# Rotating 96 images by 90 degrees: 2 MB loads of whole slabs, and neighbouring slabs stored together

## The chip, the cores and the metric

The kernel runs on one core of a Trainium2 chip. A core has a vector engine (DVE), a scalar engine (ACT), a queue engine that issues transfers (SP), and 16 DMA engines that move data between device memory (HBM) and the on-chip memory SBUF, which has 128 partitions. A second on-chip memory, PSUM, can be written and read by DVE and ACT but not by DMA. The metric is the device time of one execution in microseconds (us); less is better. A slab in this text is 2 MB of rows.

## The reference

```python
def setup_inputs():
    batch, c, h, w = 32, 3, 256, 256
    return {"x": np.random.randn(batch, c, h, w).astype(np.float32)}

def reference(x: np.ndarray) -> np.ndarray:
    return np.rot90(x, k=-1, axes=(-2, -1)).astype(np.float32)
```

Each of the 96 images of 256 x 256 float32 values is turned by a quarter clockwise. Nothing is calculated: 25.17 MB are read, put into another order, and 25.17 MB are written.

## The kernel before

The 24,576 image rows are cut into 12 slabs of 2048 rows, eight images each. All twelve slabs stay in SBUF at once, each in a *unit*: 16 KB in every one of the 128 partitions.

A transfer lays several consecutive rows of 1 KB into one partition. There are two layouts. *Short* is 8 rows, so 8 KB in one piece, and a slab is two such pieces per partition, one from each half of the slab (index `i`). *Long* is 16 rows, 16 KB in one piece; here a half of the slab goes to every second partition (`i::2`, 64 of them).

DVE's 32x32 block transpose with a rearranged source and destination (L118) does the turning, in two instructions of 128x2048 values for one slab. It turns what is read short into what is written long, and the other way round; a third form takes two units in the long layout at once, in four instructions. Slabs 0, 1 and 2 are loaded short and stored long; slabs 3 to 7 are loaded long and stored short; 8 with 9 and 10 with 11 are loaded and stored long. Slabs 1 and 2 are loaded by one transfer of 2 MB each, all others by halves of 1 MB, and the first half of slab 11 is cut once more, into 14 KB and 2 KB rows.

A turn does not write into its own unit. `home = [turned0] + units[:last]` (L100): slab n is turned from unit n into unit n-1, which the turn before has set free, and slab 0 goes to PSUM (`turned0`). At the end ACT copies `turned0` into the last unit (L146), and slab 0 is stored from there, as the last store of the program (`store(0)`, L148). The pairs 8/9 and 10/11 move likewise: the turn of the pair 8/9 writes into the tile of units 3 and 7, that of 10/11 into the tile of 8/9.

A unit is a tile of its own, except that three tiles hold two units each (L72: 3 with 7, 8 with 9, 10 with 11), so that a paired turn can address both. Waits between instructions are not written by hand: the framework derives them from which tile regions an instruction reads and writes.

All transfers are issued by SP, in program order: all loads first (L88, L92, L96), then the stores. The stores of slabs 4, 3, 5, 6, 7, 1, 2 follow, the first of them held back by hand until the 14 KB piece of slab 11's load has landed (L139), so that stores do not start among the loads. After that each paired turn is followed by its stores (L124, L127), and slab 0 comes last (L130). L124 stores slab 8 (and later 10), both halves, in one transfer of 2 MB from the 64 even partitions, two pieces of 16 KB each that lie 1 MB apart in the output; slabs 9 and 11 follow from the odd partitions in halves of 1 MB (L127). The short stores (L132) are of 2 MB, the long ones of slabs 0, 1 and 2 (L130) of 1 MB. SP has eight completion semaphores for its transfers in use, and a transfer waits until the one eight places before it has landed.

Of the kernel before, what the change touches and what calls it, by code (L numbers as in the profile page):

```python
# [1 line left out]

# [4 lines left out]

@with_exitstack
def kernel(
    ctx: ExitStack,
    tc: tile.TileContext,
    x: bass.AP,
    out: bass.AP,
):

    nc = tc.nc
    fp32 = mybir.dt.float32

    B, C, H, W = x.shape
    P = nc.NUM_PARTITIONS
    RL, RS = 16, 8  # L50
    I = 2
    Q = P * RS // H
    n_slabs = B * C // (Q * I)
    last = n_slabs - 1
    F = RS * W
    long_st = (0, 1, 2)
    both = (8, 10)
    paired = [n + a for n in both for a in range(2)]

    rows_in = x.rearrange("b c h w -> (b c h) w")  # L60
    rows_out = out.rearrange("b c h w -> (b c h) w")

    def short(rows):
        return rows.rearrange("(n i p r) w -> n p i (r w)", i=I, p=P, r=RS)

    def long(rows):
        return rows.rearrange("(n i m r) w -> n i m (r w)", i=I, m=P // I, r=RL)

    ld_short, ld_long, st_short, st_long = short(rows_in), long(rows_in), short(rows_out), long(rows_out)

    units = [None] * n_slabs
    adjacent = [(3, 7), (8, 9), (10, 11)]  # L72
    pairs = []
    for us in adjacent + [(u,) for u in range(n_slabs) if all(u not in us for us in adjacent)]:
        pool = ctx.enter_context(tc.tile_pool(name=f"unit{us[0]}", bufs=1))
        held = pool.tile([P, len(us), I * F], fp32, name=f"u{us[0]}")
        for j, u in enumerate(us):
            units[u] = held[:, j]
        pairs.append(held)
    psum = ctx.enter_context(tc.tile_pool(name="psum", bufs=1, space=bass.MemoryType.PSUM))  # L80
    turned0 = psum.tile([P, I * F], fp32, name="turned0")

    def fours(t):
        return t.rearrange("p (i f) -> p i f", i=I)

    for n in (0, 1, 2, 3, 7, 4, 5, 6, *range(8, n_slabs)):
        if n in (1, 2):
            nc.sync.dma_start(out=fours(units[n]), in_=ld_short[n])  # L88
            continue
        for i in range(I):  # L90
            if n in long_st:
                ld = nc.sync.dma_start(out=fours(units[n])[:, i], in_=ld_short[n][:, i])  # L92
            else:
                cuts = (0, 14 * W, RL * W) if (n, i) == (last, 0) else (0, RL * W)
                for f0, f1 in zip(cuts, cuts[1:]):
                    ld = nc.sync.dma_start(out=units[n][i::I, f0:f1], in_=ld_long[n, i][:, f0:f1])  # L96
                    if f1 == 14 * W:
                        mark = ld

    home = [turned0] + units[:last]  # L100

    def turn(n):
        if n in long_st:
            src = fours(units[n]).rearrange("p i (r g c) -> p c r g i", r=RS, c=RL)
            dst = home[n].rearrange("p (c k r) -> p c r k", c=RL, r=RS)[:, :, ::-1, ::-1]
            parts, step = 2, RL // 2
        elif n in paired:
            if n not in both:
                return
            src = pairs[both.index(n) + 1].rearrange("p a (r g c) -> p c r g a", r=RL, c=RL)  # L110
            dst = pairs[both.index(n)].rearrange("p i (c k r) -> p c r k i", c=RL, r=RL)[:, :, ::-1, ::-1, :]
            parts, step = 4, RL // 4
        else:
            src = units[n].rearrange("p (r g c) -> p c r g", r=RL, c=RS)
            dst = fours(home[n]).rearrange("p i (c k r) -> p c r k i", c=RS, r=RL)[:, :, ::-1, ::-1, :]
            parts, step = 2, RS // 2
        for h in range(parts):
            nc.vector.transpose(out=dst[:, h * step : (h + 1) * step], in_=src[:, h * step : (h + 1) * step])  # L118

    def store(n):  # L120
        if n in paired:
            first = n if n in both else n - 1
            if n == first:
                nc.sync.dma_start(out=st_long[n].transpose([1, 0, 2]), in_=pairs[both.index(n)][::I])  # L124
                return
            for i in range(I):
                nc.sync.dma_start(out=st_long[n, i], in_=pairs[both.index(first)][n - first :: I, i])  # L127
        elif n in long_st:
            for i in range(I):
                nc.sync.dma_start(out=st_long[n, i], in_=home[n][i::I])  # L130
        else:
            return nc.sync.dma_start(out=st_short[n], in_=fours(home[n]))  # L132

    for n in range(both[0]):
        turn(n)
    for n in (4, 3, 5, 6, 7, 1, 2):
        st = store(n)
        if n == 4:
            tc.add_manual_dep(st.ins, mark.ins.name, mybir.DependencyInfo(  # L139
                mybir.DependencyClass.Sync, mybir.DependencyReason.SCHED_ONLY), reason="stores after loads")  # L140
    for n in range(both[0], n_slabs):
        turn(n)
        store(n)

    for i in range(I):
        nc.scalar.copy(out=fours(units[last])[:, i], in_=fours(turned0)[:, i])  # L146
    home[0] = units[last]
    store(0)  # L148


# [1 line left out]
_INS = ['x']  # L152
_OUTS = [((32, 3, 256, 256), 'float32')]


# [23 lines left out]
```

## Time and profile before

| what | us |
|---|---|
| median of 3 runs | 123.27 (123.24 to 123.33) |
| span of the profiled execution | 121.4 |
| DVE busy, 24 transposes | 90.5 |
| ACT busy, two copies and a table load | 4.9 |
| first transpose starts | 8.25 |
| last stores issued | 102.8 and after |

The page gives the profiled execution by its span; the time of the runs lies about 1.8 us above it, which is launch and end outside the profile. The profile is read from left to right in time: start and length in microseconds, the engine (a `q` behind it means its queue: waits and issues of transfers, which don't count as busy), the line of the kernel, the operation, what is written `<-` what is read, and in brackets the idle time before it and what ended that. Names of tiles are without their numbers: `u` is any unit, `turned` is the PSUM tile. A row of digits is a share in tenths over 40 equal slices of the span.

### The profile page before, as it was taken

Reading aid. Unit: us, or ns where it says so; the run is one execution under the profiler, and the core shown is the slowest. Engines: PE = TensorE matmul, PEld = TensorE weight load, DVE = VectorE, ACT = ScalarE, POOL = GpSimd, SP = SyncE. Lnnn points to the kernel's source line nnn. Section 1 sums busy time; section 2 is a strip of 40 time slices with the busy share of each in tenths; the row PEclk is TensorE's granted clock in tenths of the full one; section 3 lists DMA queues with packets and bytes.
Section 4 is the critical chain, followed back from the end, with each engine's and each line's share of the span. In section 5 each row is a group of like instructions: output and inputs, shape, how many; then the busy total and the mean of one; then the engine's idle time right before and its main releaser. Section 6 shows DMA issues by size and latency. Waiting matters only on the chain.

```text
span 121.4 us, 134 instructions
## 1 busy us (share of the span) xinstructions
DVE 90.5 (75%) x24; ACT 4.9 (4%) x3; POOL 0.2 (0%) x4
## 2 busy tenths in 40 slices
DVE  0029999999999999999999999999999960000000
ACT  0000000000000000000040000000000038000000
POOL 0000000000000000000000000000000000000000
DMA  3999999999999999999999999999999999999994
GB/s 84 416 432 424 426 459 432 432 432 426 426 432 426 416 421 432 421 426 450 403 424 426 426 429 429 421 432 424 464 426 432 432 432 432 432 432 432 432 432 178
DMA packets 4800, 50.33 MB, mean 414 GB/s; under 512 B 640, under 2 KB 640, under 8 KB 704
## 3 DMA queue, kind: packets, MB, share of 16 engines
q1 hardware_dynamic: 4800, 50.33, 98.0%
HBM read 25.17 MB, written 25.17 MB: 414 GB/s over the span
## 4 chain that ended last, share of the span: by engine, by line
DVE 55%; issue 17%; DMA 6%; DVEq 3%; ACT 2%; ACTq 1%; SPq 0%
DVE u L118 50%; DVE turned L118 6%; DMA u<-in_x_dram 6%; DVEq L174 3%; ACT u L146 2%; ACTq L174 1%; SPq L92 0%; DVEq L118 0%
## 5 line engine op out<-in xcount | busy, mean ns | idle before, releaser
L118 DVE STREAM_TRANSPOSE u<-u 128x2048 f32<-128x2048 f32 x22 | 83.4, 3861 | 0.3
L118 DVE STREAM_TRANSPOSE turned<-u 128x2048 f32<-128x2048 f32 x2 | 7.1, 3584 | 8.3 <-DMA u<-in_x_dram 8.3
L146 ACT COPY u<-turned 128x2048 f32<-128x2048 f32 x2 | 3.6, 1869 | 35.6 <-DVE u L118 35.6
L146 ACT ACT_TABLE_LOAD x1 | 1.3, 1283 | 62.3 <-DMA u<-in_x_dram 62.3
L163 POOL MEMSET const-uint8-127<- 128x1 uint8 x1 | 0.1, 103 | 0.0
L163 POOL MEMSET const-bfloat16-1.0<- 128x1 bf16 x1 | 0.1, 101 | 0.0
L163 POOL MEMSET const-float32-0.0<- 128x1 f32 x1 | 0.1, 99 | 0.2 <-issue 0.2
L163 POOL MEMSET const-float32-1.0<- 128x1 f32 x1 | 0.1, 99 | 0.0
## 6 DMA issues: line engine op xcount, KB each, us to landing
u<-in_x_dram SPq DMA_DIRECT2D x19, 1024.0 KB, 19.6
out_dram<-u SPq DMA_DIRECT2D x7, 2048.0 KB, 16.3
out_dram<-u SPq DMA_DIRECT2D x10, 1024.0 KB, 18.3
u<-in_x_dram SPq DMA_DIRECT2D x2, 2048.0 KB, 13.7
u<-in_x_dram SPq DMA_DIRECT2D x1, 896.0 KB, 19.3
u<-in_x_dram SPq DMA_DIRECT2D x1, 128.0 KB, 17.2
```

The lines of the kernel that those rows point to most:

```text
L118: nc.vector.transpose(out=dst[:, h * step : (h + 1) * step], in_=src[:, h * step : (h + 1) * step])
L146: nc.scalar.copy(out=fours(units[last])[:, i], in_=fours(turned0)[:, i])
L163: nc = _bacc.Bacc("TRN2", target_bir_lowering=False, num_devices=1)
L174: with _tile.TileContext(nc) as tc:
```

## The change

Every slab is now loaded in the short layout, by one transfer of 2 MB (`ld`, 128 partitions, two pieces of 8 KB each). Units lie in six tiles of two neighbours (`pairs`). The load order starts with the last slab: unit 0 receives slab 11, and unit u receives slab u-1 for u from 1 to 11. Every unit is turned in the form that slabs 0 to 2 had, two transposes each; unit u is turned into unit u-1, so that slab u-1 ends in the unit with its own number, and unit 0 (slab 11) is turned into PSUM (`held`). ACT copies `held` into unit 11. So tile n holds the turned slabs 2n and 2n+1 side by side, and is stored long by two transfers of 2 MB, each from 64 partitions with two pieces of 16 KB, one for each slab; the two pieces lie 2 MB apart in the output. There are 12 loads and 12 stores, 24 transfers for 40. In the program all loads come first, then all turns, the copies, and the stores; the dependency written by hand (L139) is gone. The cases of `turn` and `store` go with it.

```diff
-    long_st = (0, 1, 2)
-    both = (8, 10)
-    paired = [n + a for n in both for a in range(2)]
...
+    ld = rows_in.rearrange("(n i p r) w -> n p i (r w)", i=I, p=P, r=R // I)
+    st = rows_out.rearrange("(n s i m r) w -> n i m s (r w)", s=2, i=I, m=P // I, r=R)
+    pairs = [
+        ctx.enter_context(tc.tile_pool(name=f"pair{n}", bufs=1)).tile([P, 2, E], fp32, name=f"u{n}")
+        for n in range(n_slabs // 2)
+    ]
+    units = [u[:, s] for u in pairs for s in range(2)]
+    psum = ctx.enter_context(tc.tile_pool(name="psum", bufs=1, space=bass.MemoryType.PSUM))
+    held = psum.tile([P, E], fp32, name="held")
+    for u, s in enumerate((last, *range(last))):
+        nc.sync.dma_start(out=units[u].rearrange("p (i f) -> p i f", i=I), in_=ld[s])
...
-    adjacent = [(3, 7), (8, 9), (10, 11)]
...
-    for n in (0, 1, 2, 3, 7, 4, 5, 6, *range(8, n_slabs)):
-        if n in (1, 2):
-            nc.sync.dma_start(out=fours(units[n]), in_=ld_short[n])
-            continue
...
+    for u in range(n_slabs):
+        src = units[u].rearrange("p (i r g c) -> p c r g i", i=I, r=R // I, c=R)
+        dst = units[u - 1] if u else held
+        dst = dst.rearrange("p (c k r) -> p c r k", c=R, r=R // I)[:, :, ::-1, ::-1]
+        for c in (slice(0, hw), slice(hw, R)):
+            nc.vector.transpose(out=dst[:, c], in_=src[:, c])
+    for h in range(2):
+        part = slice(h * E // 2, (h + 1) * E // 2)
+        nc.scalar.copy(out=units[last][:, part], in_=held[:, part])
...
-    for n in range(both[0]):
-        turn(n)
-    for n in (4, 3, 5, 6, 7, 1, 2):
-        st = store(n)
-        if n == 4:
-            tc.add_manual_dep(st.ins, mark.ins.name, mybir.DependencyInfo(
-                mybir.DependencyClass.Sync, mybir.DependencyReason.SCHED_ONLY), reason="stores after loads")
-    for n in range(both[0], n_slabs):
-        turn(n)
-        store(n)
-    for i in range(I):
-        nc.scalar.copy(out=fours(units[last])[:, i], in_=fours(turned0)[:, i])
-    home[0] = units[last]
-    store(0)
+    for n, u in enumerate(pairs):
         for i in range(I):
+            nc.sync.dma_start(out=st[n, i], in_=u[i::I])
```

More of the change, by code (lines that the diff above doesn't have):

```diff
@@ L49 @@
     P = nc.NUM_PARTITIONS
-    RL, RS = 16, 8
+    R = 16
     I = 2
-    Q = P * RS // H
-    n_slabs = B * C // (Q * I)
+    E = R * W
+    n_slabs = B * C * H // (P * R)
     last = n_slabs - 1
-    F = RS * W
-    long_st = (0, 1, 2)
-    both = (8, 10)
-    paired = [n + a for n in both for a in range(2)]
+    hw = R // 2
     rows_in = x.rearrange("b c h w -> (b c h) w")
     rows_out = out.rearrange("b c h w -> (b c h) w")
-    def short(rows):
-        return rows.rearrange("(n i p r) w -> n p i (r w)", i=I, p=P, r=RS)
@@ L66, in long @@
[L66 to L71, printed above, removed]
-    adjacent = [(3, 7), (8, 9), (10, 11)]
[L73 to L79, printed above, removed]
@@ L80 @@
-    psum = ctx.enter_context(tc.tile_pool(name="psum", bufs=1, space=bass.MemoryType.PSUM))
-    turned0 = psum.tile([P, I * F], fp32, name="turned0")
-    def fours(t):
-        return t.rearrange("p (i f) -> p i f", i=I)
-    for n in (0, 1, 2, 3, 7, 4, 5, 6, *range(8, n_slabs)):
-        if n in (1, 2):
-            nc.sync.dma_start(out=fours(units[n]), in_=ld_short[n])
-            continue
-        for i in range(I):
[L91 to L125, printed above, removed]
-            for i in range(I):
[L127 to L132, printed above, removed]
@@ L134 @@
-    for n in range(both[0]):
-        turn(n)
-    for n in (4, 3, 5, 6, 7, 1, 2):
-        st = store(n)
-        if n == 4:
-            tc.add_manual_dep(st.ins, mark.ins.name, mybir.DependencyInfo(
-                mybir.DependencyClass.Sync, mybir.DependencyReason.SCHED_ONLY), reason="stores after loads")
-    for n in range(both[0], n_slabs):
-        turn(n)
-        store(n)
-    for i in range(I):
-        nc.scalar.copy(out=fours(units[last])[:, i], in_=fours(turned0)[:, i])
-    home[0] = units[last]
```

## The prediction

> **What bounds the kernel now.** I read the page's shares and its forty slices first, then rates by stretch, then the order of work around the two ends, then DVE's queue around one wait.
>
> ```profile
> span 121.4 us, 134 instructions
> DVE 90.5 (75%) x24; ACT 4.9 (4%) x3; POOL 0.2 (0%) x4
> DMA  3999999999999999999999999999999999999994
> ...
> q1 hardware_dynamic: 4800, 50.33, 98.0%
> ```
>
> The DMA engines are full from the second slice to the last but one: the 50.33 MB in one queue are the bound, and DVE, busy for 75%, runs beside them. Whether a larger transfer helps is read from the rates by stretch (after the length: busy times, the clock, the DMA share, GB/s):
>
> ```profile
> 1.80:5.00 3.20, 0.00 (x0) 0.00 (x0) 0.00 (x0) 1.00 0.85 320
> ...
> 6.00:17.00 11.00, 8.71 (x3) 0.00 (x0) 0.00 (x0) 1.00 1.00 425
> 20.00:56.00 36.00, 35.83 (x10) 0.00 (x0) 0.00 (x0) 1.00 1.01 429
> 63.00:81.00 18.00, 17.97 (x6) 0.55 (x1) 0.00 (x0) 1.00 1.01 428
> 87.00:118.00 31.00, 12.07 (x4) 3.63 (x2) 0.00 (x0) 1.00 1.01 431
> ```
>
> In order: the cold start; loads in 8 KB rows, in transfers of 2 MB; loads in 16 KB rows, of 1 MB; stores in 8 KB rows, of 2 MB; stores in 16 KB rows, of both sizes. The four steady rates lie within 1.4% of each other. What else could set the end is the chain of DVE, ACT and the last stores (timeline):
>
> ```profile
> 8.25 7.08 DVE L118 STREAM_TRANSPOSE turned<-u 128x2048 f32<-128x2048 f32 x2 [8.25 <-DMA u<-in_x_dram]
> 15.36 83.70 DVE L118 STREAM_TRANSPOSE u<-u 128x2048 f32<-128x2048 f32 x22
> ...
> 99.10 3.63 ACT L146 COPY u<-turned 128x2048 f32<-128x2048 f32 x2 [35.56 <-DVE u L118]
> ...
> 102.76 2.67 SPq L130 DMA_DIRECT2D out_dram<-u  x2
> ```
>
> DVE starts when slab 0 is there and then never waits: one chain of 24 transposes from 8.25 to 99.1. The last 2 MB wait for it and for ACT's two copies, but are issued at 102.8 and land near 120.6 in a queue that still holds earlier stores. So a delay of DVE's start would show at the end as soon as it is larger than that reserve. What DVE's first turn must wait for is therefore the question, and one place in the trace tells what a turn waits for (timeline of SP, then DVE's queue, in narrow windows):
>
> ```profile
> 18.11 0.47 SPq L96 DMA_DIRECT2D u<-in_x_dram  x1
> ...
> 25.45 0.47 SPq L96 DMA_DIRECT2D u<-in_x_dram  x1
> ...
> 27.89 0.47 SPq L96 DMA_DIRECT2D u<-in_x_dram  x1
> ```
> ```profile
> L118 DVEq EVENT_SEMAPHORE  x1: 50/50/50, 25.5 to 25.5; - x1
> ...
> L118 DVEq EVENT_SEMAPHORE  x1: 50/50/50, 27.9 to 27.9; - x1
> ```
>
> From the ninth load on, SP issues one each time that the load eight places earlier has landed, so its issues are a list of landings. Unit 2 landed at 18.1; then come halves of 1 MB every 2.45 us: unit 3 at 20.6 and 23.0, unit 7 at 25.4 and 27.9. DVE's queue passes waits at 18.1 (for unit 2), at 25.5 and 27.9, and next at 32.8 (for unit 4). The only turn between those of units 2 and 4 is that of unit 3. Had it waited only for its own load, its wait would have passed by 23.0; it passed with the landings of unit 7, which that turn neither reads nor writes. What units 3 and 7 share is a tile: held[P, 2, 4096]. The wait cost nothing, since DVE was still busy with unit 2 until 31.07.
>
> **The change, part by part.**
>
> *Tiles of two.* Every unit now has a neighbour in a tile of just that shape, units 0 and 1 among them. If a turn waits for the loads of both, DVE's first turn starts after the second 2 MB load and no longer after the first. Loads of that form landed at 8.17, 13.14 and 18.11. Before, DVE started 0.08 after the landing; so now at 13.22 for 8.25, 4.97 later. All later turns have cover: unit u lands at about 8.2 + 4.95u and is turned from 20.3 + 7.86(u-1) on, so the pair of units 2 and 3 (landed by 23.1) is needed at 28.2.
>
> *DVE's forms.* 24 transposes of 128x2048 stay. All take the form that slabs 0 to 2 have now: two into PSUM, 7.11 from start to start (8.25 to 15.36), then eleven turns like those of units 1 and 2, which run from 15.36 to 31.07, 7.855 each, 86.4 in all for 83.74 now. The last eight transposes of before took about 3.69 each and go up to 3.93; that is the 2.7. DVE ends at 13.22 + 7.11 + 86.4 = 106.7 (without the new wait 101.8).
>
> *ACT.* The same two copies, 3.63, then SP issues 0.03 later: the last pair's first store is issued at 110.4 (105.5). ACT's table load is long over by then.
>
> *The last pair.* Both 2 MB stores of pair 5 hold rows of unit 11, so both wait for ACT; before, slab 11's store did not. After the issue come 4.19 MB at 431 GB/s, 9.73 us, and a start and landing latency, which no row shows for a store into an empty queue. The nearest is the first load: 4.9 from issue to landing of 1 MB, less 2.45 of streaming, leaves 2.45. Of that 0.81 is the slow first stretch (320 GB/s for 3.2 us in place of 428), which may belong to a cold start alone, so 1.65 to 2.45. SP's first closing drain is at 120.7, and a pair whose stores are to land by then must be issued by 120.7 - 9.73 - 2.45 = 108.5 to 109.3. At 110.4 it is 1.1 to 1.9 late; DMA idles for about as long between pairs 4 and 5. I take 1.35, nearer the lower end, because this is a restart after a short pause.
>
> *The Trainium skill on the fixed cost.* "DMA: Bandwidth & Descriptors", section on the anatomy of one DMA, gives about 2.0 us fixed per transfer (fitted on GpSimd's path), and its rules for kernel authors advise to coalesce. By that, 16 transfers fewer would be worth up to 32 us if they stood one behind the other. The rows say otherwise while the queue is full: 1 MB loads land 2.45 us apart, which is 428 GB/s with nothing over. At the one place where the queue runs empty the page's figure would make the lateness 1.4, inside the bounds above.
>
> *Bytes and rows.* The bytes stay. 9 slabs (18.87 MB) of loads go from 16 KB to 8 KB rows: at 429 and 425 GB/s that is 43.99 to 44.40, +0.4 at most, and nothing if the first window was still unsettled. 5 slabs (10.49 MB) of stores go the other way, 428 to 431: 24.50 to 24.33, -0.17. The stream alone is thus -0.2 to +0.2, middle 0. With the new wait the end is set by the chain, and this lies beside it.
>
> *Issues.* SP issues 24 transfers for 40. A 2 MB load took 0.43 to 0.92 to issue, the 2 MB form of L124 0.63; all lie beside a full queue but the last two, counted above. The stores' held-back start (SP waits 13.9 and 10.9 us at L132 and L124 now) goes; the twelve loads are issued by about 23, the first store waits for turn 2 (36.0) and queues behind them. Eight transfers may be in flight, and the last stores wait for those of pair 1, landed before 85: free. Pair 4 is ready at 98.9 and, by the same sum with 19.46 us still to send, needed by 98.8 to 99.6: just covered, and what it may be late lies inside the lateness of pair 5.
>
> *Pitch.* [...] In this trace L124's stores, with 1 MB between their halves, run inside the 431 GB/s stretch, and I charge nothing.
>
> Sum, against the profiled span: 121.4 + 1.35 = 122.8; the median of the runs, 123.27, lies 1.8 above that span, so **124.6**.
>
> **The rivals.**
>
> *No new wait (not slower).* If a turn waits only for its own unit, DVE starts at 8.25, the last pair is issued at 105.5, 3 us before its limit of 108.5, and the stream alone counts: 123.1 to 123.5, taken 123.2. For it: ACT's copies into unit 11 did not have to wait for anything of unit 10 that a row shows. Against it: unit 3's turn, the same instruction on a tile of the same shape. It decides at a start delay of 3.0: any less and nothing shows at the end.
>
> *8 KB loads slower over the whole phase.* SP's issues put the landings of such loads 4.97 apart, against 4.89 for two 16 KB halves; held for 9 more slabs that is +0.7, and with the stores' gain 123.8 without the new wait. With it the late chain covers the same 0.7 and the time stays at 124.6. Against it: 425 GB/s over eleven microseconds leaves room for less.
>
> *Paired stores slower.* Their halves lie 2 MB apart, as no transfer of before has it. At 410 GB/s in place of 431 the 25.17 MB would take 61.4 us for 58.4, and the stream alone gives 126.3 with or without the wait. Against: the L124 row, with 1 MB between.
>
> **How the numbers follow.** A new wait: 0.72, with 124.6 and its own range 124.2 to 125.3 (lateness 0.9 to 2.0). No new wait: 0.19. Slower loads without the wait: 0.05. Slower paired stores: 0.04. Range 123.0 to 125.4, which leaves out the last case and the edges. No change is what lies within 0.2%, 0.25 us, about what a measurement of this kernel can tell. Of the 0.19, 0.06 falls under 123.0 and 0.13 within; all others are slower: 0.81.
>
> **What would show it.** Right: DVE's first transpose starts at about 13.2 with 13.2 of idle time before it, released by the load; DVE ends near 106.7; ACT's copies end near 110.4; a slice near 110 to 112 in which the DMA share drops; the last SP drain 1.1 to 1.9 later. Wrong: a first transpose at 8.25 and a full DMA row to the end (then 123.2); or a steady rate of paired stores below 425 GB/s, or of loads below 422. The prediction falls if the restart costs nothing at all or if turns of unit 1's form run faster beside stores than the 7.855 seen beside loads.

## The result, and the profile after

The changed kernel takes 123.72 us (median of 5 runs, 123.66 to 123.81) for 123.24 (5 runs, 123.18 to 123.33) of the kernel before on the same chip: ratio 1.0043, 95% interval 1.0032 to 1.0053. It is slower by 0.48 us, not by the 1.35 foretold.

The page of the changed kernel, its shares, slices and queue:

```profile
span 122.0 us, 115 instructions
...
DVE 93.0 (76%) x24; ACT 4.9 (4%) x3; POOL 0.2 (0%) x4
...
DMA  4999999999999999999999999999999999999994
...
q1 hardware_dynamic: 4992, 50.33, 98.1%
```

The DMA row is full up to the end: there is no pause before the last pair. The timeline of the changed kernel says why:

```profile
8.30 7.08 DVE L57 STREAM_TRANSPOSE held<-u 128x2048 f32<-128x2048 f32 x2 [8.30 <-DMA u<-in_x_dram]
15.41 86.30 DVE L57 STREAM_TRANSPOSE u<-u 128x2048 f32<-128x2048 f32 x22
...
63.02 1.28 ACT L60 ACT_TABLE_LOAD   x1 [63.02 <-DMA u<-in_x_dram]
101.75 3.63 ACT L60 COPY u<-held 128x2048 f32<-128x2048 f32 x2 [37.44 <-DVE u L57]
```

DVE starts at 8.30, as before (8.25), and not at 13.22. The wait for the neighbour's load isn't there. DVE's chain is longer by the new form of the turns, ends at 101.7 for 99.1, ACT at 105.4, and all that is hidden, as the rival without a wait had it.

So the time must lie in the stream. ACT's table load is released by the landing of the last load, and SP's first closing drain follows the landing of the last store; the two cut the span in a load part and a store part. Of the kernel before (timeline, then SP's closing instructions):

```profile
62.26 1.28 ACT L146 ACT_TABLE_LOAD   x1 [62.26 <-DMA u<-in_x_dram]
```
```profile
L174 SPq DRAIN  x3: 7/7/7, 120.7 to 121.0; - x3
```

and SP's closing instructions of the kernel after:

```profile
L90 SPq DRAIN  x3: 7/7/7, 121.2 to 121.5; - x3
```

The last load lands 0.76 later (63.02 for 62.26). The stores then take 58.2 for 58.4. The sum is +0.5, which is the whole difference. The loads are all in 8 KB rows now. Their rate by stretch, in the changed kernel (stretch, length, busy times of DVE, ACT and POOL, clock, DMA share, GB/s):

```profile
6.00:17.00 11.00, 8.67 (x3) 0.00 (x0) 0.00 (x0) 1.00 1.02 429
20.00:56.00 36.00, 35.83 (x10) 0.00 (x0) 0.00 (x0) 1.00 1.01 422
64.00:118.00 54.00, 37.57 (x10) 3.94 (x3) 0.00 (x0) 1.00 1.01 431
```

The middle row is the loads' steady rate: 422 GB/s, where 16 KB loads ran at 429 in the same stretch before. The first row, the same kind of load, shows 429. A stretch counts a packet's bytes when the packet starts; landings come later. They were slow from the start, as the waits of DVE's queue for units 1 and 2 show:

```profile
L57 DVEq EVENT_SEMAPHORE  x2: 21/21/21, 13.3 to 18.2; - x2
```

The first load lands by 8.30, the next two by 13.3 and 18.2, the twelfth by 63.02: 11 in 54.7 us, 4.975 each. In the kernel before, SP's issues already put the loads of units 0, 1 and 2 at 8.17, 13.14 and 18.11, 4.97 apart. The same loads show 425, 427 and 427 GB/s from 6 to 17 us in three of the runs below (e1, e5 and e6), so a stretch of eleven microseconds tells their rate only to a few GB/s.

### The profile page after: what moved, and what is told of

Its sections match the earlier page's. It is cut to its first block, busy times and chain, and to the rows that moved or that the text cites. A ratio compares the mean times of both kernels' runs of the same rounds, so it can differ in the third digit from the quotient of the medians.

```text
span 122.0 us, 115 instructions
## 1 busy us (share of the span) xinstructions
DVE 93.0 (76%) x24; ACT 4.9 (4%) x3; POOL 0.2 (0%) x4
## 4 chain that ended last, share of the span: by engine, by line
DVE 44%; issue 29%; DMA 6%; DVEq 3%; ACT 2%; ACTq 1%
DVE u L57 39%; DMA u<-in_x_dram 6%; DVE held L57 6%; DVEq L90 3%; ACT u L60 2%; ACTq L90 1%
## 5 line engine op out<-in xcount | busy, mean ns | idle before, releaser
L57 DVE STREAM_TRANSPOSE u<-u 128x2048 f32<-128x2048 f32 x22 | 86.0, 3985 | 0.4
L57 DVE STREAM_TRANSPOSE held<-u 128x2048 f32<-128x2048 f32 x2 | 7.1, 3587 | 8.3 <-DMA u<-in_x_dram 8.3
L60 ACT COPY u<-held 128x2048 f32<-128x2048 f32 x2 | 3.6, 1869 | 37.4 <-DVE u L57 37.4
```

Source lines behind the costliest of these rows:

```text
L57: nc.vector.transpose(out=dst[:, c], in_=src[:, c])
L60: nc.scalar.copy(out=units[last][:, part], in_=held[:, part])
```

## Experiments

Runs e1 to e6 start from the changed kernel, e7 to e10 from the kernel before. Times of experiments are compared with runs of the kernel before on the same chip (123.31 for the first four, 123.22 for the next three, 123.25 for the last three).

| run | loads | us | ratio to before, interval | first turn | last load landed | closing drain |
|---|---|---|---|---|---|---|
| before | 16 KB rows, three slabs 8 KB | 123.24 | 1 | 8.25 | 62.26 | 120.7 |
| after | 8 KB rows | 123.72 | 1.0043 (1.0032 to 1.0053) | 8.30 | 63.02 | 121.2 |
| e1_halves | 8 KB, 1 MB each | 123.91 | 1.0047 (1.0033 to 1.0060) | 8.26 | - | 121.4 |
| e2_rows16k | 16 KB | 123.23 | 0.9998 (0.9988 to 1.0008) | 8.41 | 62.27 | 120.6 |
| e3_rows4k | 4 KB | 126.15 | 1.0226 (1.0206 to 1.0247) | 8.59 | 64.94 | 123.2 |
| e4_firstlong | 8 KB, first two slabs as unit 3 before | 124.96 | 1.0129 (1.0115 to 1.0143) | 13.54 | 63.20 | 122.5 |
| e5_noturn | 8 KB, no turns | 123.94 | 1.0062 (1.0047 to 1.0077) | none | - | 121.5 |
| e6_stores4k | 8 KB, stores in 4 KB | 125.28 | 1.0167 (1.0150 to 1.0184) | 8.29 | 63.03 | 122.8 |

(A dash: no instruction that marks the landing of the whole last load.)

**Is it the transfer or its rows? e1_halves.**

```diff
-        nc.sync.dma_start(out=units[u].rearrange("p (i f) -> p i f", i=I), in_=ld[s])
+        for i in range(I):
+            nc.sync.dma_start(out=units[u].rearrange("p (i f) -> p i f", i=I)[:, i], in_=ld[s][:, i])
```

> Each slab's load in two transfers of 1 MB instead of one of 2 MB, the same 8 KB rows in the same places. The changed kernel's loads land 4.97 us apart per slab, 16 KB loads of before 4.89. Theory A, the row length costs (8 KB rows need twice as many packets): nothing changes, 4.97 per slab, 123.7 us. Theory B, the cost lies in one transfer that steps between two pieces 1 MB apart: the rate comes back, 4.89 per slab, 12 x 0.075 = 0.9 less, 122.8 us.

The first turn of this run and its rates by stretch:

```profile
8.26 7.08 DVE L58 STREAM_TRANSPOSE held<-u 128x2048 f32<-128x2048 f32 x2 [8.26 <-DMA u<-in_x_dram]
```
```profile
6.00:17.00 11.00, 8.71 (x3) 0.00 (x0) 0.00 (x0) 1.00 1.01 425
20.00:56.00 36.00, 35.83 (x10) 0.00 (x0) 0.00 (x0) 1.00 1.01 422
```

Measured: 123.91 us; the stretch from 20 to 56 shows 422 GB/s as in the changed kernel. Theory B falls: that a transfer steps between two pieces 1 MB apart costs nothing, and twelve more transfers in a full queue change the time by less than these runs resolve (1.0047 for 1.0043). The second result of this run: its first turn starts at 8.26, with two transfers per unit and a neighbour in the tile.

**e2_rows16k.**

```diff
-    ld = rows_in.rearrange("(n i p r) w -> n p i (r w)", i=I, p=P, r=R // I)
+    ld = rows_in.rearrange("(n p r) w -> n p (r w)", p=P, r=R)
...
-        nc.sync.dma_start(out=units[u].rearrange("p (i f) -> p i f", i=I), in_=ld[s])
+        nc.sync.dma_start(out=units[u], in_=ld[s])
```

> Each slab's load stays one transfer of 2 MB to 128 partitions, but with one row of 16 KB per partition instead of two pieces of 8 KB. The rows so lie in other partitions than the turns assume, so the output is a permuted one; all sizes, turns and stores are those of the changed kernel. Theory A (row length): 4.89 per slab, 122.8 us, faster than before by about 0.4 us because all stores run at 4.86. Theory C, loads into all 128 partitions or of 2 MB are slower whatever their rows, as all 16 KB loads of before were of 1 MB into every second partition: 4.97 per slab, 123.7 us.

The timeline of this run and its rates by stretch:

```profile
8.41 7.08 DVE L57 STREAM_TRANSPOSE held<-u 128x2048 f32<-128x2048 f32 x2 [8.41 <-DMA u<-in_x_dram]
...
62.27 1.28 ACT L60 ACT_TABLE_LOAD   x1 [62.27 <-DMA u<-in_x_dram]
```
```profile
20.00:56.00 36.00, 35.83 (x10) 0.00 (x0) 0.00 (x0) 1.00 1.01 429
64.00:118.00 54.00, 37.70 (x10) 3.63 (x2) 0.00 (x0) 1.00 1.01 431
```

With only the row length changed the last load lands at 62.27 for 63.02 and the rate is 429 for 422: (62.27 - 8.41)/11 = 4.90 per slab, as theory A had it, and theory C falls. The gain in the whole is smaller than foretold: the span shrinks by 0.7 (122.0 to 121.3), the ratio by 0.0045, 0.55 us, for an expected 0.9; 0.1 of what is missing is the first load, which lands 0.11 later than in the changed kernel. It was also expected to be 0.4 faster than the kernel before, and ties with it (0.9998), though all its loads run at 429 and all its stores at 431. So 16 KB rows on both sides bring back what the change lost, and no more.

**e3_rows4k.**

```diff
-    ld = rows_in.rearrange("(n i p r) w -> n p i (r w)", i=I, p=P, r=R // I)
+    ld = rows_in.rearrange("(n i p r) w -> n p i (r w)", i=4, p=P, r=R // 4)
...
-        nc.sync.dma_start(out=units[u].rearrange("p (i f) -> p i f", i=I), in_=ld[s])
+        nc.sync.dma_start(out=units[u].rearrange("p (i f) -> p i f", i=4), in_=ld[s])
```

> The load in four pieces of 4 KB per partition, else as the changed kernel; the output is a permuted one. Theory A with a fixed cost per packet: a 16 KB packet takes 2447/4 = 612 ns of an engine, an 8 KB packet 4970/16 = 310.6, so 9 ns per further packet; a 4 KB packet 160 ns, 5.12 us per slab, 12 x 0.15 = 1.8 us more than the changed kernel, 125.5 us. Theory A without a fixed cost per packet, only a bad pairing of 8 KB pieces: no more than 123.7 us.

Rates by stretch of this run:

```profile
20.00:56.00 36.00, 35.83 (x10) 0.00 (x0) 0.00 (x0) 1.00 1.03 410
64.00:118.00 54.00, 37.91 (x10) 4.92 (x3) 0.00 (x0) 1.00 1.01 432
```

(64.94 - 8.59)/11 = 5.12 per slab, the number foretold. The three row lengths lie nearly on one line: from 16 to 8 KB each engine has 8 packets more per slab and needs 0.079 us more, 9.9 ns each; from 8 to 4 KB 16 more and 0.148, 9.2 ns each. The closing drain is 2.0 later than in the changed kernel for a foretold 1.8. The runs scatter (125.70 to 126.49), and the profiled one is the fastest; their median, 126.15, lies above the 125.5 foretold.

**The wait that was foretold. e4_firstlong.**

```diff
+    ld_long = rows_in.rearrange("(n i m r) w -> n i m (r w)", i=I, m=P // I, r=R)
...
     for u, s in enumerate((last, *range(last))):
+        if u < 2:
+            for i in range(I):
+                nc.sync.dma_start(out=units[u][i::I], in_=ld_long[s, i])
+            continue
         nc.sync.dma_start(out=units[u].rearrange("p (i f) -> p i f", i=I), in_=ld[s])
```

> The first two slabs are loaded in halves of 1 MB with 16 KB rows into every second partition, as unit 3 and unit 7 were before; everything else as in the changed kernel. The rows of these two slabs lie in other places than the turns assume, so the output is a permuted one there. Theory D, a turn waits for its neighbour's load too when the loads go to every second partition: the first transpose starts at about 13.1 and not 8.3, DVE ends at 106.5, the last pair is issued at 110.3. With the recorded price (start and landing 1.65 to 2.45 on top of 9.73) the last landing is at 121.7 to 122.5 against 121.2 in the changed kernel: 124.2 to 125.1 us. If the restart costs less than 1.1, the wait is there and the end is hidden: 123.6 us. Theory E, the wait of unit 3's turn had another cause than the form of the loads: first transpose at 8.2, 123.6 us.

DVE's queue at the start of this run, then the timeline, and the rates around the pause:

```profile
L62 DVEq EVENT_SEMAPHORE  x2: 21/36/50, 11.0 to 13.4; - x2
L62 DVE STREAM_TRANSPOSE held<-u x2: 3564/3585/3606, 13.5 to 17.1; 128x2048 f32<-128x2048 f32 x2
...
  DMA u<-in_x_dram: 13.5, 1
```
```profile
107.01 3.63 ACT L65 COPY u<-held 128x2048 f32<-128x2048 f32 x2 [42.54 <-DVE u L62]
110.67 1.25 SPq L69 DMA_DIRECT2D out_dram<-u  x2
```
```profile
107.00:112.00 5.00, 0.00 (x0) 3.63 (x2) 0.00 (x0) 1.00 0.82 351
112.00:120.00 8.00, 0.00 (x0) 0.00 (x0) 0.00 (x0) 1.00 1.00 424
```

Theory D holds. The first turn passes its waits at 11.0 and 13.4, with the landings of unit 1, which it doesn't touch, and starts at 13.54. The chain then runs as the prediction put it: the last pair is issued at 110.67 (foretold 110.4), DMA falls to 0.82 of its share around it, and the closing drain comes at 122.5. From issue to drain less 9.73 of streaming are 2.1 us, inside the 1.65 to 2.45 that were charged. So the wait is real, its price lay within the bounds, and the changed kernel doesn't have it, because its loads go to all 128 partitions. That it is the alternate partitions, and not two transfers or 16 KB rows, follows with e1 (two transfers, no wait, 8.26) and e2 (16 KB rows, no wait, 8.41); two transfers of 16 KB rows to all partitions were not run.

**Do the transposes slow the loads? e5_noturn.** The loop of turns and ACT's copies are left out; every unit is stored as loaded.

```diff
-        for c in (slice(0, hw), slice(hw, R)):
-            nc.vector.transpose(out=dst[:, c], in_=src[:, c])
...
-        nc.scalar.copy(out=units[last][:, part], in_=held[:, part])
```

> The changed kernel without turns and without ACT's copies: every unit is stored as it was loaded, so only the transfers are left. Theory A (the row length costs the DMA engines): loads still land 4.97 us apart, stores 4.86, 123.7 us. Theory F, the 8 KB loads are slowed by the transposes that write and read SBUF beside them, and 16 KB loads less so: 4.89 per slab, 122.8 us.

```profile
20.00:56.00 36.00, 0.00 (x0) 1.00 1.01 422
64.00:118.00 54.00, 0.00 (x0) 1.00 1.01 431
```

Without any DVE work (here the columns are POOL, clock, DMA share and GB/s) the rates are the same two numbers. Theory F falls. The run also shows that the changed kernel is bound by its stream alone: 123.94 us with nothing else in it.

**Do stores pay for their rows too? e6_stores4k.**

```diff
-    st = rows_out.rearrange("(n s i m r) w -> n i m s (r w)", s=2, i=I, m=P // I, r=R)
+    st = rows_out.rearrange("(n s i p r) w -> n s p i (r w)", s=2, i=4, p=P, r=R // 4)
...
-            nc.sync.dma_start(out=st[n, i], in_=u[i::I])
+            nc.sync.dma_start(out=st[n, i], in_=u[:, i].rearrange("p (i f) -> p i f", i=4))
```

> The changed kernel with stores of one unit each in four pieces of 4 KB per partition from all 128 partitions, 2 MB per transfer as before; the output is a permuted one. Loads as in the changed kernel. If a further packet costs a store as much as a load, 9 ns, a 4 KB store takes 4.86 + 24 x 0.009 = 5.08 per unit, 2.6 us more in all: 126.3 us. By the 8 KB stores of before, 4.873 for 4.862, a further packet costs a store 1.4 ns at most: 4.90 per unit, 0.4 more, 124.1 us.

```profile
20.00:56.00 36.00, 35.83 (x10) 0.00 (x0) 0.00 (x0) 1.00 1.01 422
64.00:118.00 54.00, 37.60 (x10) 3.94 (x3) 0.00 (x0) 1.00 1.02 421
```

Neither number was met. From the last load to the drain are 59.8 us for 58.2, 1.6 more over 12 units and 24 further packets per engine and unit: 5.6 ns per packet, between the 1.4 and the 9 that were offered. This run also stores from all partitions rather than every second one, so the 5.6 isn't the row length alone beyond doubt.

**A version without 8 KB loads: e7, e8, e9, e10.** If 8 KB loads cost 0.075 per slab and 8 KB stores 0.01, the kernel before should gain by loading slabs 0 to 2 long and storing them short.

```diff
-    long_st = (0, 1, 2)
+    long_st = ()
...
-        if n in (1, 2):
-            nc.sync.dma_start(out=fours(units[n]), in_=ld_short[n])
-            continue
```

> The kernel before with slabs 0, 1 and 2 loaded in 16 KB rows and stored in 8 KB rows, like slabs 3 to 7, so that no load is in 8 KB rows. By theory A the three loads gain 3 x 0.075 = 0.23 and the three stores lose 3 x 0.01: 123.1 us for 123.3. If the first loads are bounded by their start and not by their rows, the gain is smaller, 0.1 or none. The new turn of slab 0 needs the same two transposes; DVE's chain gets no longer.

Measured: 124.29 us, ratio 1.0086 (1.0071 to 1.0101): a clear miss. DVE's chain is longer too, against the expectation: ACT's copy follows it at 99.79 for 99.10, beside a queue that stays full. The last load lands at 62.26, no earlier than in the kernel before (the first turn starts 0.13 later, at 8.38, which eats a part of the gain), and the stores take 59.4 for 58.4. Two parts of it and a repetition, with `long_st = (0,)` (e8), `long_st = (1, 2)` (e9) and the same program on another chip (e10):

> The kernel before with only slabs 1 and 2 loaded in 16 KB rows and stored in 8 KB rows; slab 0 as before. The version with all three was 1.0 us slower, and its stores, not its loads, took the time: 59.3 us from the last load's landing to the last store's for 58.5 in the kernel before. If the short stores of slabs 1 and 2 bring that, this one is slower by 0.5 or more; if it is slab 0, stored last, or only that chip, it is 123.1 us.

> The kernel before with only slab 0 loaded in 16 KB rows and stored, as the last one, in 8 KB rows. If slab 0 brings the slower stores, this one is slower by 0.5 or more, with packets of 616 ns among the stores in place of 611; if slabs 1 and 2 do, it is 123.2 us.

> The version with all three slabs in 16 KB rows once more. If its slower stores belong to the program, 124.3 us again with store packets of 615 ns; if to the chip or the place of the output in memory, 123.1 us.

Measured: e8 123.59 us, 1.0029 (1.0020 to 1.0038); e9 123.53, 1.0025 (1.0016 to 1.0034); e10 124.36, 1.0092 (1.0075 to 1.0109). The slowdown belongs to the program, not to a chip. Of e8 and e9 neither met a case that was offered: both were to be either 0.5 or more slower, or not slower at all. e8's loads gain what they should (last landing 62.00 for 62.26), and its stores lose more: 58.9 for 58.4. Rates of the store part, one row each of the kernel before, e7, e8 and e9:

```profile
64.00:118.00 54.00, 35.00 (x10) 3.63 (x2) 0.00 (x0) 1.00 1.01 430
64.00:118.00 54.00, 35.69 (x10) 3.63 (x2) 0.00 (x0) 1.00 1.01 426
64.00:118.00 54.00, 34.90 (x10) 3.63 (x2) 0.00 (x0) 1.00 1.01 428
64.00:118.00 54.00, 35.72 (x10) 3.63 (x2) 0.00 (x0) 1.00 1.01 430
```

e9's stores take 58.5, so it did not bring the slow stores; it loses 0.2 before the last load lands (62.44). In the traces' packet records the 16 KB stores that start after 90 us take 615 ns on average in e7 and e8, for 611 in the kernel before and in e9. Why seven slabs in short stores, or eight, slow also the later long stores, while five or six don't, stays open: the records show the longer packets and not their cause. No version beat the kernel before.

## Why the prediction was wrong

That the kernel came out slower, as forecast, and within the stated 123.0 to 125.4, is luck: the wait that was to make it slower isn't there, and a term put at about nothing made it slower instead.

**Tiles of two: the step that failed.** The prediction read the wait of unit 3's turn as one for the whole tile, and put DVE's first turn at 13.22; it starts at 8.30. The reading of the row was right, and the rule drawn from it was too wide. The row had a second feature, the loads into every second partition, and the prediction called the new place "a tile of just that shape" and did not ask whether the loads had the same form. e1, e2 and e4 separate the features: neighbours in one tile wait for each other's loads if these go to every second partition, and not if they go to all. The wait is set by the framework's derivation of dependencies, not by the chip.

**ACT, the last pair: right.** Where the wait exists (e4), the issue at 110.67 and the 2.1 us of start and landing met the foretold 110.4 and 1.65 to 2.45.

**DVE's forms: right.** Eleven turns took 86.3 (foretold 86.4), DVE ended at 101.7 (foretold 101.8 for no wait). The 2.5 us more of DVE are hidden.

**Bytes and rows: mis-sized.** The term was put at -0.2 to +0.2 beside everything else, and with the wait gone it is the whole result: +0.76 of loads and -0.2 of stores. The error was to take 425 GB/s from a stretch of eleven microseconds right behind the cold start, with "nothing if the first window was still unsettled". It was unsettled the other way: the changed kernel shows 429 in that stretch and 422 after it, for the same loads, while the landings were 4.97 apart from the first one. The prediction had the 4.97 and gave the case of slow loads without the wait a chance of 0.05, at 123.8; measured 123.72. Its main case without the wait stood at 123.2. The argument against it, "425 GB/s over eleven microseconds leaves room for less", is what fell. Why 8 KB rows are slower is settled as far as a price per packet in loads (9 to 10 ns, three row lengths nearly on one line, the same with halved transfers and without DVE); what in the engine takes these nanoseconds no run shows.

**Issues and the fixed cost: right.** No gain from 24 transfers for 40 shows in a full queue; e1, with twelve transfers more, agrees. The loads were not issued by about 23, as forecast: SP's issues of them run to 35.0 (12 from 0.73 on, the longest 10.9 us), which the full queue hides. That a transfer pays a start and a landing of its own shows only where the queue ran empty, in e4, at 2.1 us. This is close to the 2.0 that the Trainium skill's "DMA: Bandwidth & Descriptors", section on the anatomy of one DMA, gives for transfers issued by GpSimd; here SP issues them.

**Pitch: right.** The pair stores, 2 MB between their halves, run at 431 GB/s. The Trainium skill's "DMA: Bandwidth & Descriptors", section on latency and other measured facts, reports 164 GB/s for copies between HBM tensors with a pitch of 2 MiB from partition to partition, where the full rate is 214. That loss does not show here, where neighbouring partitions lie 16 KB apart and only the two halves of a transfer 2 MB.

## What to carry to other kernels

In a kernel that fills its DMA queue, count packets and not transfers: e1's split transfers changed nothing, halving the rows of the loads cost 9 to 10 ns per further packet and engine. Take a stream's rate from landings over a long stretch: eleven microseconds of packets right behind the start gave 425 to 429 GB/s for loads that land at 422. And when one row shows a wait, list every feature of the instructions in it before carrying it over; here the shape of the tile was the wrong one of two.

## What was not expected of the hardware

Loads and stores do not price rows alike: from 16 to 4 KB rows the loads' rate falls from 429 to 410 GB/s, the stores' from 431 to 421, and e6's stores also go out from all partitions instead of every second one. And the stores of two programs that differ only in how slabs 0 to 2 are loaded, turned and stored differ by 1 us in 58 (e7 and the kernel before), again on a second chip (e10), with the later 16 KB stores slowed too; this is unexplained.
